# Hybrid SSD and GLA trunk, block 0: the third and the fourth GLA gate are projected in two steps instead of one

## The chip, the cores and the metric

The kernel runs on one core of a Trainium2 chip. The metric is the device time of one execution in microseconds (us), lower is better. Engines are named as in the profile: PE is the matrix engine, PEld its weight loads, DVE the vector engine, ACT the scalar engine, POOL the GpSimd engine, SP the engine that issues most of the DMAs.

## The reference

The reference is one decoder layer over 16 learned meta tokens and 2048 real tokens, width 1024, in float32. Cut to what matters here:

```python
u = rmsnorm(hres, norm_w)
proj = jnp.einsum('bld,dn->bln', u, w_in)
z, xbc, dt_raw, q, k, v, g_gla, a_lr, merge_g = split_cols(proj, IN_WIDTHS)
# branch 1 (SSD): short causal convolution and silu of xbc, chunked scan of 16 heads in 4 groups,
#                 times silu(z), RMSNorm per group
# branch 2 (GLA): 4 heads of gated linear attention in chunks
gate_logit = jnp.einsum('blr,rk->blk', a_lr, gla_gate_w2) + gla_gate_b
log_a = (jax.nn.log_sigmoid(gate_logit.astype(jnp.float32)) / GLA_GATE_TEMP)
# inside gla_chunked: gc = cumsum of log_a within a chunk
merged = jnp.sum(gates * branch_proj, axis=2)
return hres + jnp.einsum('bld,de->ble', merged, w_out)
```

The change concerns `gate_logit`: a rank-16 product per GLA head, its log-sigmoid and the cumulative sum in chunks.

## The kernel before, in words

The 2048 tokens are worked in four blocks of 512; block 0 also carries the 16 meta tokens (`m0` = 16), so it is 528 wide and most of its products are cut into two segments of 264 columns. Every large product is three matmuls (L214, L215, L216 in `accum`), because each operand is held as a high and a low part. After the blocks come the merge gates, the branch products and the output product; the change does not touch those.

Inside a block the work is a chain of **pieces**, and a piece is one projection or a half of one. For block 0 the chain is: `proj_zm` (steps 0 and 1), the convolution tiles of group 0 (steps 2 to 5), the z columns of group 1 in two halves (6, 7), the four convolution tiles of group 1 (8 to 11), z of group 2 (12, 13), the convolution tiles of group 2 (14 to 17), and so on; below, z of group 2 is the third z group. After each piece, `step()` advances every running generator by one `yield`: `gates` from step 6 on, and an `ssd_scan` for each group from steps 6, 12, 18 and 24 on. `gates` comes ahead of the scans in that list. The GLA scans that read the gates' result begin at step 30.

The order of instructions on PE and on the SP queue is this program order (`manual_schedule`). The order on DVE, ACT and POOL is chosen by the scheduler of the Tile framework when the kernel is built, and is then fixed; every engine works its queue in order. `tc.issue_after(x)` ties instructions behind `x` on their engine.

The accumulators lie in eight banks, in three pools: `pj` with three, `pt` with three and `pc` with two. What the steps around the change use:

- `proj_conv` (L585): one convolution tile takes two `pj` banks, one per segment. ACT evicts each bank twice (L595 into `cin`, L596 into `acc`), DVE adds three taps (L600), ACT takes a tanh (L603), DVE multiplies (L604). The matmuls of one tile run through both banks in turn.
- `proj_z` (L577): two `pj` banks over two steps; ACT takes the tanh of a bank (L516), DVE multiplies (L517).
- `gates` (L468): per head and segment one matmul (L488) with 48 rows, into a `pj` bank for the first segment and a `pt` bank for the second, each evicted by DVE (L490) and by ACT (L491). After a pair of heads come Exp (L493) and Ln (L494) over both, and then for each head a subtraction (L498) and the scans (L500). In block 0 these last are put off to the end of the step and tied behind the newest convolution tap or decay product (`convd`).
- `ssd_scan` (L618): `before(c)` transposes chunk `c` into a `pt` bank (L664), DVE takes three products from it (L667 to L670), ACT builds the decay (L677, L679), DVE masks it (L680). `after(c)`, one step later, multiplies with it on PE (L689, then L690 and L692 in two `pc` banks), and DVE adds up (L695 to L702). Step 11 runs `before(3)` and `after(2)` of group 0, step 12 `after(3)`; step 13 begins group 1's scan (L632, L648, L664).

Before the change, `gates` runs heads 0 and 1 together in step 7, and heads 2 and 3 together in step 11.

Of the kernel before, what the change touches and what calls it, by code (L numbers as in the profile page):

```python
# [43 lines left out]
def trunk_kernel(ctx: ExitStack, tc: tile.TileContext, xm, xmt, w_feat, w_tok, w_v3, w_zm, w_br, w_o,  # L44
# [7 lines left out]
    def mk(pool, shape, dt, tag, **kw):  # L52
        cnt[0] += 1
        return pool.tile(shape, dt, tag=tag, name=f"{tag}_{cnt[0]}", **kw)
# [77 lines left out]
    def bank(pool, tag):  # L132
        return mk(pool, [P, 512], F32, tag)
# [334 lines left out]
    def gates(o):  # L468
        m0, tt, chunks, g_all = o.m0, o.tt, o.chunks, o.g_all
        ast = (mk(wk, [P, META + BLK], F32R, "act", bufs=NACT) if m0 else mk(wk, [P, BLK], F32R, "sq", bufs=NSQ))[:48, :tt]  # L470
        for a, n in ([(0, META), (m0, BLK)] if m0 else [(0, BLK)]):
            ps = bank(pt, "pt")
            for i, (ca, cn) in enumerate(chunks):
                if a <= ca < a + n:
                    nc.tensor.transpose(ps[:48, ca - a:ca - a + cn], o.alr[:cn, i], ident[:cn, :cn])
            nc.scalar.activation(ast[:, a:a + n], ps[:48, :n], AF.Copy)
            nc.vector.tensor_tensor(ast[:32, a:a + n], ps[:32, :n], ast[:32, a:a + n].bitcast(F32),
                                    op=ALU.subtract)
            nc.scalar.activation(ast[:16, a:a + n], ps[:16, :n], AF.Copy)
        yield  # L480
        for h2 in range(0, GH, 2):
            gmt = mk(wk, [P, 2, META + BLK], F32, "tok4", bufs=NT4)
            for h in (h2, h2 + 1):
                gm = gmt[:, h % 2, :tt]
                gb = gate_b[:, h:h + 1]
                for i, (a, n) in enumerate(o.segs_all):
                    ps = bank(*((pj, "pj") if m0 and i == 0 else (pt, "pt")))
                    nc.tensor.matmul(ps[:, :n], w2[:, h * P:(h + 1) * P], ast[:, a:a + n],  # L488
                                     start=True, stop=True)
                    nc.vector.tensor_scalar(gm[:, a:a + n], ps[:, :n], gb, 0.0, op0=ALU.add, op1=ALU.min)  # L490
                    evicted[:] = [nc.scalar.activation(g_all[:, h, a:a + n], ps[:, :n], AF.Abs, bias=gb)]  # L491
            ga = g_all[:, h2:h2 + 2, :tt]
            nc.scalar.activation(ga, ga, AF.Exp, scale=-1.0)  # L493
            nc.scalar.activation(ga, ga, AF.Ln, bias=1.0)  # L494
            yield
            for h in (h2, h2 + 1):
                def sums(h=h):
                    nc.vector.tensor_tensor(gmt[:, h % 2, :tt], gmt[:, h % 2, :tt], g_all[:, h, :tt], op=ALU.subtract)  # L498
                    for a, n in chunks:
                        nc.vector.tensor_tensor_scan(g_all[:, h, a:a + n], ones[:, :n], gmt[:, h % 2, a:a + n], 0.0,  # L500
                                                     op0=ALU.mult, op1=ALU.add)

                if m0:
                    put_off.append(sums)
                else:
                    sums()
                yield
            if m0 and not h2:
                yield
# [494 lines left out]
    def enter(pieces, o):  # L1004
        b = o.b
        total = 6 * (SG + GH) + (b == nblk - 1)
        for n in range(total + 1):
            i, r = divmod(n, 6)
            if r == 0:
                if i == 1 and b == 0:  # L1010
                    begin(gates(o))
                if 0 < i <= SG:
                    begin(ssd_scan(o, i - 1))
                elif i > SG and not (b == nblk - 1 and i - SG > LATE_G):
                    begin(gla_scan(o, i - SG - 1))
                if (b, i) in beside:
                    begin(beside_unit(beside[b, i]))
            if b and n == 7:
                begin(gates(o))
            if n == 6 * SG + (3 if b else 0):  # L1020
                begin(fetch_u(b + 1) if b + 1 < nblk else first_b())
            if n < total:
                yield next(pieces)
        assert next(pieces, pieces) is pieces
# [502 lines left out]
```

## Time and profile before

| | |
|---|---|
| median of 3 runs | 2242.24 us (2240.61 to 2245.01) |
| the profiled execution | 2246.45 us, of which the span of the trace is 2244.7 us |
| PE busy | 2211.9 us, 99% of the span |
| DVE, ACT, POOL busy | 70%, 53%, 31% |
| mean granted clock of PE | 0.997 |
| DVE in block 0, from 90 to 110 us | 19.99 of 20 us |

PE's share is near the whole span, so what matters is where PE stands idle or runs slowly, and who makes it wait. In rows of the timeline the columns are start (us), duration (us), engine, line, operation, tiles written and read, and shapes; the brackets hold the idle time of the engine before the instruction and what ended it.

### The profile page before, as it was taken

The numbers are of one execution on the slowest core, as the hardware profiler recorded it, in microseconds if no ns is written. First come the engines' busy times: TensorE is split into PE (matmuls) and PEld (weight loads), VectorE is DVE, ScalarE is ACT, GpSimd is POOL, SyncE is SP. The second block draws the span as 40 slices with busy tenths as digits, with TensorE's granted clock in tenths as the row PEclk, the third lists the DMA queues.
The fourth block names the chain that finished last, engine by engine and source line by source line (L and its number), as shares of the span: only waits on it lengthen the run. The fifth ranks groups of instructions, "written<-read, shape, count | busy, mean of one in ns | idle before, by whom it ended". The sixth has DMA issues, their size and how long they took to land.

```text
span 2244.7 us, 34971 instructions
## 1 busy us (share of the span) xinstructions
PE 2211.9 (99%) x11789; PEld 1896.8 (85%) x11789; DVE 1577.0 (70%) x2935; ACT 1187.0 (53%) x2767; POOL 693.9 (31%) x689
## 2 busy tenths in 40 slices
PE   7999999999999999999999999999999999999998
PEld 7999999888888888888988888878888888888887
DVE  5775676677557676567677666674679945789866
ACT  5666655575445456544465544454644545454544
POOL 5444433223212122221212100066233374324341
PEclk9999999999999999999999999999999999999999
DMA  9767875767777667778667664376768866787753
GB/s 313 247 222 234 273 259 202 237 209 240 240 244 260 212 213 237 241 245 272 207 212 233 213 211 160 127 250 198 241 227 289 303 221 217 237 282 245 261 177 121
DMA packets 313699, 517.95 MB, mean 231 GB/s; under 512 B 28080, under 2 KB 162480, under 8 KB 313520
## 3 DMA queue, kind: packets, MB, share of 16 engines
q1 hardware_dynamic: 247008, 419.89, 57.8%
q10 hardware_dynamic: 65872, 93.74, 11.5%
q8 instruction: 92, 1.51, 0.3%
q0 software_dynamic: 640, 2.10, 0.2%
q14 instruction: 87, 0.71, 0.1%
HBM read 368.42 MB, written 147.19 MB: 230 GB/s over the span
## 4 chain that ended last, share of the span: by engine, by line
PE 89%; DVE 4%; DMA 3%; ACT 2%; issue 1%; POOL 1%; SPq 0%; POOLq 0%; ACTq 0%; DVEq 0%
PE pj L214 20%; PE pj L216 20%; PE pj L215 19%; PE pt L215 4%; PE pt L214 4%; PE pt L216 4%; PE pc L689 2%; PE pc L214 2%; PE pc L216 2%; PE pc L215 2%; PE pc L850 2%; PE pc L690 1%; DMA acc<-in_xmt 1%; PE pc L692 1%; PE pc L958 1%
## 5 line engine op out<-in xcount | busy, mean ns | idle before, releaser
L214 PE MATMUL pj<-ue,whl 128*128 128x264 f32 (+1 forms) x672 | 235.3, 350 | 1.9 <-ACT acc L596 1.2
L216 PE MATMUL pj<-ue,whl 128*128 128x264 f32 (+1 forms) x672 | 229.7, 342 | 0.0
L215 PE MATMUL pj<-ue,whl 128*128 128x264 f32 (+1 forms) x672 | 228.8, 340 | 0.0
L214 PE MATMUL pj<-uo,whl 128*128 128x512 f32 x512 | 205.7, 402 | 0.0
L216 PE MATMUL pj<-uo,whl 128*128 128x512 f32 x512 | 200.1, 391 | 0.0
L215 PE MATMUL pj<-uo,whl 128*128 128x512 f32 x512 | 199.5, 390 | 0.0
L214 PE MATMUL pj<-b,a 128*128 128x512 f32 (+1 forms) x484 | 188.9, 391 | 0.7 <-DVE io L1252 0.5
L216 PE MATMUL pj<-b,a 128*128 128x512 f32 (+1 forms) x484 | 188.9, 390 | 0.3 <-DVE a L1134 0.3
L215 PE MATMUL pj<-b,a 128*128 128x512 f32 (+1 forms) x484 | 187.6, 388 | 0.0
L600 DVE SCALAR_TENSOR_TENSOR acc<-cin,hcw,acc 128x512 f32<-128x512 f32 (+1 forms) x192 | 156.7, 816 | 39.7 <-ACT acc L596 38.6
L83 POOL TENSOR_TENSOR wr<-wr 128x256 f32<-128x256 f32 x80 | 66.0, 826 | 371.8 <-DMA wr<-y 158.1
L1124 POOL TENSOR_TENSOR as<-ar,ar 128x512 f32<-128x512 f32 x40 | 62.9, 1572 | 374.7 <-DMA ar<-in_w_br 179.9
L1134 DVE TENSOR_TENSOR a<-ar,a 128x512 fp32r<-128x512 f32 x160 | 130.8, 824 | 65.0 <-ACT a L1133 63.5
L1109 DVE TENSOR_TENSOR b<-br,b 128x512 fp32r<-128x512 f32 x140 | 128.9, 943 | 18.1 <-ACT b L1108 17.8
L214 PEld LDWEIGHTS pj<-ue,whl 128*128 128x128 f32 x672 | 126.2, 188 | 17.7 <-ACT acc L596 1.7
L216 PEld LDWEIGHTS pj<-ue,whl 128*128 128x128 f32 x672 | 126.4, 188 | 14.9
L215 PEld LDWEIGHTS pj<-ue,whl 128*128 128x128 f32 x672 | 126.4, 188 | 14.7
L177 POOL TENSOR_TENSOR whl<-wr,whl 128x512 fp32r<-128x512 f32 (+1 forms) x76 | 96.9, 1282 | 126.2 <-ACT whl L175 94.4
L1168 ACT ACTIVATE sn<-pj 128x512 f32<-128x512 f32 x118 | 70.0, 593 | 123.8 <-PE pj L216 70.8
L1134 DVE TENSOR_TENSOR a<-as,a 128x512 fp32r<-128x512 f32 x120 | 101.6, 848 | 45.2 <-ACT a L1133 42.5
L1133 ACT ACTIVATE a<-ar 128x512 fp32r<-128x512 f32 x160 | 99.0, 624 | 64.7 <-PE pt L216 30.2
L215 PE MATMUL pt<-b,a 128*128 128x512 f32 x320 | 125.6, 392 | 3.9 <-DVE b L1109 3.9
(329 smaller groups left out, 6467.6 us busy)
## 6 DMA issues: line engine op xcount, KB each, us to landing
whl<-k_s SPq DMA_DIRECT2D x96, 512.0 KB, 3.7
whl<-k_g SPq DMA_DIRECT2D x96, 512.0 KB, 4.3
whl<-k_v SPq DMA_DIRECT2D x36, 512.0 KB, 4.0
wr<-in_w_feat SPq DMA_DIRECT2D x64, 256.0 KB, 4.5
k_s<-whl SPq DMA_DIRECT2D x32, 512.0 KB, 3.9
cb<-cumd SPq DMA_DIRECT2D x64, 256.0 KB, 5.1
y<-gg ACTq DMA_DIRECT2D x64, 256.0 KB, 4.2
k_g<-whl SPq DMA_DIRECT2D x32, 512.0 KB, 4.0
```

The source lines that it names most:

```text
L83: nc.gpsimd.tensor_tensor(o, x, y, op=ALU.subtract)
L177: nc.gpsimd.tensor_tensor(hl[:, 1], raw, hl[:, 0].bitcast(F32), op=ALU.subtract)
L214: nc.tensor.matmul(ps, sh, mh, start=first, stop=False, **kw)
L215: nc.tensor.matmul(ps, sh, ml, start=False, stop=False, **kw)
L216: nc.tensor.matmul(ps, sl, mh, start=False, stop=last, **kw)
L600: convd[:] = [nc.vector.scalar_tensor_tensor(acc, cin[:, k:k + tt], hcw[:, ti, k:k + 1], acc, op0=ALU.mult, op1=ALU.add)]
L689: nc.tensor.matmul(py[:, h * 64:(h + 1) * 64], dm[:, h], xdt[:, h], start=True, stop=True)
L1109: nc.vector.tensor_tensor(t[:, 1], raw, t[:, 0].bitcast(F32), op=ALU.subtract)
L1124: nc.gpsimd.tensor_tensor(s1, a21, a22, op=ALU.add)
L1133: nc.scalar.activation(t[:, 0], src, AF.Copy)
L1134: latest[:] = [nc.vector.tensor_tensor(t[:, 1], src, t[:, 0].bitcast(F32), op=ALU.subtract)]
L1168: nc.scalar.activation(sn, self.ps[n, "a"], AF.Copy)
```

## The change

One `yield` is added in `gates`, which is reached in block 0 alone, between head 2 and head 3. Head 2 stays in step 11; head 3's matmuls and evictions, and the Exp and Ln over the pair, go to step 12; the put-off sums of heads 2 and 3 go from steps 12 and 13 to steps 13 and 14. No instruction is added or taken away.

```diff
                     nc.vector.tensor_scalar(gm[:, a:a + n], ps[:, :n], gb, 0.0, op0=ALU.add, op1=ALU.min)
                     evicted[:] = [nc.scalar.activation(g_all[:, h, a:a + n], ps[:, :n], AF.Abs, bias=gb)]
+                if m0 and h == 2:
+                    yield
             ga = g_all[:, h2:h2 + 2, :tt]
             nc.scalar.activation(ga, ga, AF.Exp, scale=-1.0)
             nc.scalar.activation(ga, ga, AF.Ln, bias=1.0)
```

## The prediction

> **What bounds the kernel now.** I read three views in this order: the matrix engine's (PE's) waits over the whole span, PE's timeline around the only long one in the first block, and the busy time and granted clock in the stretches of 3.41 us in which the clock changed. First the waits, longest in total on top: who waited and for whom, us in total, times, longest.
>
> ```profile
> core 0 of [0], span 2244.7 us
> engine line waited for: us in total, times, longest us
> PE pt L324 <- DMA cst<-in_cf: 10.1, 1, 10.1
> PE pt L215 <- DVE b L1109: 3.9, 3, 1.7
> PE pj L488 <- ACT acc L596: 3.1, 1, 3.1
> ```
>
> Behind the start-up load of 10.1 us PE hardly waits at all, so PE's own queue sets the end, and a microsecond that PE loses in block 0 is lost at the end. The third row is the one that the change touches. L488 is the gate matmul of `gates`, and it waits once in the kernel, for the eviction L596 of a convolution. PE's timeline (start, duration, line, tile, in brackets the idle time before it) shows which matmul, and what it costs behind it:
>
> ```profile
> 107.58 0.58 PE L488 MATMUL pj<-act,w 48*128 48x264 f32 x1 [3.15 <-ACT acc L596]
> ...
> 108.32 0.90 PE L664 MATMUL pt<-cst,act 128*128 128x128 f32 x3
> 109.01 1.80 PE L689 MATMUL pc<-c,sq 128*128 128x64 f32 x8
> ...
> 112.07 0.78 PE L214 MATMUL pj<-whl,ue 128*128 128x256 f32 x1
> ```
>
> This is step 11 (fourth convolution tile of group 1), then step 12 (first half of the third z group). In step 11 head 2's two matmuls run at once, in the third `pj` bank. Head 3's first matmul needs the first bank of the convolution tile that PE has only just finished, and stands from 104.43 to 107.58. Why that bank is late, on the scalar engine (ACT):
>
> ```profile
> 105.54 0.64 ACT L603 ACTIVATE act<-acc 128x528 f32<-128x528 f32 x1 [2.17 <-DVE acc L600]
> ...
> 106.97 0.56 ACT L596 ACTIVATE acc<-pj,hcb,hcw 128x264 f32<-128x264 f32 x1
> ...
> 107.69 0.58 ACT L596 ACTIVATE acc<-pj,hcb,hcw 128x264 f32<-128x264 f32 x1
> ```
>
> ACT works in order and was held by the tanh L603 of the tile before, which waited 2.17 us for the vector engine (DVE). Only then came the eviction of the first bank (ends 107.53) and of the second (ends 108.27). Now the clock (stretch, its length, busy time and count of PE, PEld, DVE, ACT, POOL, granted PE clock, DMA share, GB/s):
>
> ```profile
> 103.15:106.56 3.41, 1.29 (x10) 0.93 (x8) 3.41 (x8) 1.24 (x4) 0.00 (x0) 1.00 0.63 206
> 106.56:109.98 3.42, 2.40 (x11) 2.17 (x11) 3.41 (x7) 3.42 (x10) 2.83 (x3) 0.50 0.07 24
> 109.98:113.39 3.41, 3.41 (x13) 3.05 (x14) 3.24 (x8) 3.41 (x10) 1.26 (x2) 0.50 0.97 318
> ```
>
> The stall costs twice. After a stretch in which PE worked 1.29 of 3.41 us, the clock is 0.50 until 113.39. From 107.58 to 113.39 PE works 5.81 us at half speed, so about 2.9 us more are lost. The price of this place today is 3.15 + 2.9 = 6.05 us. Note also that DVE is busy for the whole of the first two stretches: behind PE's stall stands a full DVE.
>
> **The change, part by part.** The added `yield` leaves head 2 in step 11. Head 3's two matmuls, its two DVE evictions L490, its two ACT evictions L491, and the pair's Exp and Ln go to step 12, behind the first half of the third z group; the two sums go one step later too. `gates` issues no DMA, so no queue of SP or POOL is passed. Nothing is added or removed, only the order.
>
> *Step 11.* At 104.43 PE goes on to the three transposes L664; their `pt` bank was last used two transposes earlier. At half clock L664 to L689 took 109.01 - 108.32 = 0.69, so 0.35 at full clock: L689 could start at 104.78. It needs the decay tile that DVE finishes in L680:
>
> ```profile
> 105.76 0.68 DVE L680 TENSOR_TENSOR sq<-sq,sq 128x512 f32<-128x512 f32 x1
> ...
> 108.20 0.49 DVE L490 TENSOR_SCALAR tok<-pj,pv 128x264 f32<-128x264 f32 x1
> 108.61 0.48 DVE L490 TENSOR_SCALAR tok<-pt,pv 128x264 f32<-128x264 f32 x1
> 109.02 1.74 DVE L600 SCALAR_TENSOR_TENSOR acc<-cin,hcw,acc 128x528 f32<-128x528 f32 x1
> ...
> 115.20 0.68 DVE L680 TENSOR_TENSOR sq<-sq,sq 128x512 f32<-128x512 f32 x1
> ```
>
> The first L680 ends at 106.44 and stands in DVE's queue ahead of all that moves. So the wait of 3.15 us is not removed, it shrinks to 106.44 - 104.78 = 1.66 us at the next instruction group. Does an idle time of 1.66 us still cost the clock? The nearest rows are two later waits of 1.7 us (the L1109 row above), each in a stretch of its own:
>
> ```profile
> 1478.70:1482.10 3.40, 1.68 (x7) 1.05 (x6) 3.40 (x3) 2.44 (x5) 3.40 (x3) 1.00 0.59 196
> 1482.10:1485.50 3.40, 1.69 (x8) 1.35 (x8) 3.40 (x5) 0.00 (x0) 1.20 (x1) 1.00 0.31 85
> ```
>
> PE was busy for half of each, and the clock stayed at 1.00. I take it that the clock stays: 3.15 + 2.9 becomes 1.66. At full clock, the state product from L689 to the next projection and a half of z take, from the next step:
>
> ```profile
> 118.56 1.00 PE L689 MATMUL pc<-c,sq 128*128 128x64 f32 x8
> ...
> 120.12 0.47 PE L214 MATMUL pj<-whl,ue 128*128 128x256 f32 x1
> ...
> 126.00 0.49 PE L632 MATMUL pt<-cst,act 128*16 128x128 f32 x3
> ...
> 127.46 0.37 PE L214 MATMUL pj<-ue,whl 128*128 128x264 f32 x1
> ```
>
> 1.56 us and 5.88 us. So step 12 starts at 106.44 + 1.56 = 108.00 instead of 112.07, with its first bank evicted (107.53), and its first half of z ends at 113.88.
>
> *Step 12.* Head 3's pair took 108.32 - 107.58 = 0.74 at half clock, 0.37 at full, in the bank that head 2 left long before: 114.25. Then L689 of the last chunk, which stood at 118.56. PE would be 4.3 us early, but it needs the second L680 (115.20, end 115.88), and DVE has been full all the way. What moves that one forward: the two L490 of head 3 (0.82 us from 108.20 to 109.02) leave their place, but L600 cannot start before the second convolution eviction at 108.27, so 0.7 us are won; I allow another 0.15 for a small POOL wait on that path, which PE's earlier finish removes. L680 then ends at about 115.0. If the queue keeps head 3's L490 ahead of it, it ends at 115.88 as now; if its own inputs let it move further up, PE's 114.25 counts. Gain at this point: 2.7, 3.55 or 4.3 us. I take 3.6, because the rows tie L680 to DVE's queue and not to PE; the idle time left here is 0.7 us, less than the harmless 1.7.
>
> *Step 13 and 14.* The second half of z follows 1.56 us later and ends 5.88 us after that, at about 122.4. The convolution of group 2 begins 127.46 - 126.00 = 1.46 us behind it. Its banks are now both of z's, where before one was head 3's: with three banks taken in turn, removing head 3 from its place shifts z from banks 1 and 2 to 0 and 1, and the convolution again starts at 0. So its second bank has to be free a few tenths after 123.9. What stands in the way there:
>
> ```profile
> 126.19 0.60 ACT L516 ACTIVATE tok<-pj 128x512 f32<-128x512 f32 x1
> 126.86 0.67 DVE L517 SCALAR_TENSOR_TENSOR tok<-tok,pj 128x512 f32<-128x512 f32 x1
> ```
>
> Today the last bank of z is free at 127.53, 0.07 us after the convolution begins, and the convolution touches its second bank only after three matmuls. The cover is thin but there; I cost it at nothing, up to 0.5 us if the queues keep this order. The scans, 3.2 us of DVE each pair member, leave DVE's full stretch for one where it has idle time; their readers come in step 30. Gain 3.6 us, bounds of the working 2.0 to 4.3.
>
> The profiled execution took 2246.45 us (span 2244.7); the sum gives 2242.85 for it. The runs' median is 2242.24, 4.2 us lower, so I carry the difference over: 2238.6 us.
>
> **A rule weighed.** The Trainium skill (TensorE: Matmul & The Clock Gate, section "Part 1: The HAM clock gate") says that the clock falls to half after at least one whole idle window of about 3.4 us, and that the window runs freely and does not start with the kernel. Here it fell after a window in which PE was busy for 38%, so the trace does not bear out the first half; by it the stall would cost 3.15 us alone and the gain would be 0.85. The second half cannot be seen in one trace.
>
> **The rivals.**
> *No half clock in the timed runs.* If the stretches of 3.41 us fall so that the stall of 3.15 us is cut into two parts of less than 1.7 each, the clock stays. Then before reaches L689 of the last chunk at 107.58 + 0.37 + 0.35 + 1.56 + 5.88 = 115.74, held to 115.9 by L680, against 115.0 after: gain 0.9, 2241.3 us. Against it: only a small part of the positions does that, and this trace has the drop.
> *More than the forecast.* If L680's place moves up with PE, or the clock's low stretch lies wholly behind the stall in the usual run (6.83 us at half speed cost 3.4 and not 2.9), the gain goes to 4.3 + 0.5 = 4.8, and to the whole 6.05 if neither new wait comes: 2236.2 to 2237.4.
> *Slower: z's second bank.* The scalar engine's order is free, and head 3's Exp and Ln now come due between z's two tanhs:
>
> ```profile
> L494 ACT ACT_TABLE_LOAD  x8: 1283/1283/1283, 78.8 to 1193.5; - x8
> L494 ACT ACTIVATE g_all<-g_all x8: 1062/1062/1087, 80.1 to 1194.8; 128x1024 f32<-128x1024 f32 x6, 128x1056 f32<-128x1056 f32 x2
> ```
>
> Exp, table load, Ln and the load back are 1.06 + 1.28 + 1.06 + 1.28 = 4.7 us. Put behind the first tanh (PE is through with that bank at 119.5), they let the second start at 125.0 and free the bank at 126.3; PE wants it at about 124.3. Idle 2.0 us, more than the harmless 1.7, so 2.9 us at half clock may follow: 4.9 lost against 3.6 won, 2243.5 us. With a pair's scans of 3.2 us ahead of L517 too, 5.2 us are idle, 8.1 lost: 2246.7. It decides from a free second bank later than about 125. Against it: ACT had idle time before both tanhs, and the scans are tied behind a later L680.
> *The edit does nothing* is excluded: PE's order is the program's.
>
> **How the numbers follow.** Forecast 0.54, more 0.18, no half clock 0.10, slower 0.18. A measurement of this kernel tells about 0.2% (4.5 us) from no change; the line lies at 2237.76. The forecast's 3.6 is under it, but the low clock's position (up to 0.5 more) and the 4.3 bound reach it, and the rest of the schedule is planned anew around it; I put 0.22 of its 0.54 beyond the line. With "more" that is 0.40 faster. Of the slower case I put 0.15 beyond the line. The rest, 0.32 + 0.10 + 0.03 = 0.45, is the same. The range runs from the far end of "more", with 1 us for the spread of the runs, to the near end of the slower case: 2235.2 to 2243.5; outside lie most of the slower case and a little below.
>
> **What would show it.** Right: no wait of L488 for L596 any more; a wait of about 1.7 us of L689 for L680 in step 11 and one under 1 us in step 12; no stretch at 0.50 near 107; step 12 starting about 4 us earlier and the convolution of group 2 about 3.6. Wrong: a wait of L214 in the first matmuls of the group 2 convolution for L516 or L517, a clock of 0.50 there, or a second L680 that still ends at 115.9.

## The result and the profile after

| | before | after |
|---|---|---|
| median | 2242.07 us of 22 runs (2240.21 to 2245.01) | 2239.38 us of 22 runs (2236.72 to 2241.49) |
| profiled execution | 2246.45 us, span 2244.7 | 2241.24 us, span 2239.5 |
| PE idle at the place of the change | 3.15 us | 1.56 us |
| head 2's first gate matmul to the first projection of group 2 | 23.53 us | 19.65 us |

The ratio of after to before is 0.9986, 95% interval [0.998, 0.9992]: a gain of about 3.1 us (1.8 to 4.5). It is clear of zero, and under the 0.2% that the prediction called a measurable difference. One run of before, taken beside three of the later kernels, was in a slow state (5084.73 us) and is left out of their ratios. Two added lines push every later line number up by two: L596 of before is L598 of after, L689 is L691, L680 is L682, L516 and L517 are L518 and L519.

The distance in the last row of the table is used in all that follows. It begins with the last pair of matmuls ahead of the change (head 2's first L488: 103.93 before, 102.78 after) and ends where step 14 begins (127.46 and 122.43). So it leaves out the start of the kernel, which differs by 1.15 us between these two executions, and also a wait inside step 14.

PE's waits after, longest in total on top (who waited for whom, us in total, times, longest):

```profile
PE pt L324 <- DMA cst<-in_cf: 10.0, 1, 10.0
PE pt L215 <- DVE b L1111: 3.1, 2, 1.7
PE pc L214 <- DVE c L948: 2.6, 4, 0.8
PE pc L691 <- DVE sq L682: 1.6, 1, 1.6
```

No gate matmul waits for a convolution's eviction any more. In its place stands one wait of 1.6 us of the state product L691 for the decay tile L682. PE's timeline after:

```profile
102.78 0.39 PE L488 MATMUL pj<-act,w 48*128 48x264 f32 x1
103.01 0.28 PE L488 MATMUL pt<-act,w 48*128 48x264 f32 x1
103.22 0.55 PE L666 MATMUL pt<-cst,act 128*128 128x128 f32 x3
105.32 1.10 PE L691 MATMUL pc<-c,sq 128*128 128x64 f32 x8 [1.56 <-DVE sq L682]
...
107.00 0.47 PE L214 MATMUL pj<-whl,ue 128*128 128x256 f32 x1
...
112.97 0.39 PE L488 MATMUL pj<-act,w 48*128 48x264 f32 x1
113.19 0.28 PE L488 MATMUL pt<-act,w 48*128 48x264 f32 x1
113.40 1.10 PE L691 MATMUL pc<-c,sq 128*128 128x64 f32 x8
```

Head 3's pair now runs at 112.97 behind the first half of z, and neither it nor the L691 behind it waits. The two L682 of DVE, and what stands between them:

```profile
104.59 0.68 DVE L682 TENSOR_TENSOR sq<-sq,sq 128x512 f32<-128x512 f32 x1
...
106.95 0.41 DVE L669 TENSOR_TENSOR c<-pt,tkd 128x256 f32<-128x256 f32 x1
107.28 0.41 DVE L671 TENSOR_TENSOR c<-pt,wde 128x256 f32<-128x256 f32 x1
107.61 0.41 DVE L672 TENSOR_TENSOR tok<-pt,pv 128x256 f32<-128x256 f32 x1
107.94 1.66 DVE L602 SCALAR_TENSOR_TENSOR acc<-cin,hcw,acc 128x528 f32<-128x528 f32 x1
...
112.25 0.68 DVE L682 TENSOR_TENSOR sq<-sq,sq 128x512 f32<-128x512 f32 x1
112.85 0.41 DVE L704 TENSOR_TENSOR tok<-c,tok 128x256 f32<-128x256 f32 x1
```

The first ends at 105.27, and 0.05 us later L691 starts: that wait belongs to DVE's queue. Behind the gate's two L490 stand now the three products from the last chunk's transposes, ahead of the tap L602, where before the tap came first; and L704, which as L702 of before stood ahead of the second decay tile, stands behind it. Now the clock, in the stretches of 3.41 us in which the wait lies (columns as in the prediction). The clock does not change here, so the stretches are counted back, in steps of 3.413 us, from its fall at 2234.61, behind the last matmul:

```profile
101.28:104.69 3.41, 2.49 (x18) 1.97 (x17) 3.41 (x9) 1.12 (x3) 0.00 (x0) 1.00 0.83 270
104.69:108.10 3.41, 2.78 (x20) 2.68 (x21) 3.41 (x9) 3.41 (x10) 2.13 (x3) 1.00 0.00 0
```

The boundary at 104.69 cuts the idle time in two, PE worked 73% of the first stretch and 81% of the second, and the clock stayed at 1.00. In this execution, then, the place got 3.88 us shorter: 1.59 us less idle time, and 2.3 us for the most part from the half clock that is gone.

### The profile page after: what moved, and what is told of

Same layout as the page of the kernel before. It is cut to its first block, busy times and chain, and to the rows that moved or that the text cites. A ratio compares the mean times of both kernels' runs of the same rounds, so it can differ in the third digit from the quotient of the medians.

```text
span 2239.5 us, 34970 instructions
## 1 busy us (share of the span) xinstructions
PE 2209.3 (99%) x11789; PEld 1894.2 (85%) x11789; DVE 1577.6 (70%) x2935; ACT 1187.4 (53%) x2767; POOL 694.8 (31%) x689
## 4 chain that ended last, share of the span: by engine, by line
PE 86%; DMA 6%; DVE 4%; ACT 2%; issue 1%; SPq 1%; POOL 0%; POOLq 0%; ACTq 0%; DVEq 0%
PE pj L214 19%; PE pj L216 19%; PE pj L215 19%; PE pt L215 4%; PE pt L214 4%; PE pt L216 4%; PE pc L691 2%; PE pc L214 2%; PE pc L216 2%; PE pc L215 2%; PE pc L852 2%; DMA acc<-in_xmt 2%; PE pc L692 1%; DMA br<-gate_t 1%; PE pc L694 1%; PE pc L960 1%
## 5 line engine op out<-in xcount | busy, mean ns | idle before, releaser
L602 DVE SCALAR_TENSOR_TENSOR acc<-cin,hcw,acc 128x512 f32<-128x512 f32 (+1 forms) x192 | 158.3, 824 | 39.6 <-ACT acc L598 38.3
L1136 DVE TENSOR_TENSOR a<-as,a 128x512 fp32r<-128x512 f32 x120 | 107.1, 894 | 46.3 <-ACT a L1135 43.3
L1111 DVE TENSOR_TENSOR b<-br,b 128x512 fp32r<-128x512 f32 x140 | 123.6, 906 | 19.8 <-ACT b L1110 19.0
```

The costliest lines, as they stand in the source:

```text
L602: convd[:] = [nc.vector.scalar_tensor_tensor(acc, cin[:, k:k + tt], hcw[:, ti, k:k + 1], acc, op0=ALU.mult, op1=ALU.add)]
L1111: nc.vector.tensor_tensor(t[:, 1], raw, t[:, 0].bitcast(F32), op=ALU.subtract)
L1136: latest[:] = [nc.vector.tensor_tensor(t[:, 1], src, t[:, 0].bitcast(F32), op=ALU.subtract)]
```

## The experiments

Theory: the gain comes from the place of head 3's matmuls in PE's queue; they no longer wait for a bank, and the clock is spared. Rivals: it comes from the relief of DVE and ACT in the full stretch; or the half clock is without weight in the usual run.

### Only the later work of ACT and DVE is moved

```diff
+            if m0 and h2:
+                yield
             ga = g_all[:, h2:h2 + 2, :tt]
```

> The kernel before, with only the Exp, the Ln and the two put-off sums of heads 2 and 3 one step later; all four gate matmuls stay together in step 11. Theory (the gain comes from the matmul's place on PE): the wait of 3.1 us of the gate matmul for the convolution's eviction and the half clock stay, distance 23.5, time as before within 0.5 us. Rival (the gain comes from taking ACT and DVE work out of the full stretch): the distance falls by 1 us or more, the time by as much.

The ratio to before is 1.0000 [0.9992, 1.0009], and PE's wait stands as it was:

```profile
PE pj L488 <- ACT acc L598: 3.1, 1, 3.1
```

Moving Exp, Ln and the sums alone brings nothing that can be measured. The distance was 22.45 us and not 23.53, with the same idle time: here the clock was at 0.50 for one stretch of 3.41 us, and in the profile of before for two. Half of 3.41 is 1.7 us; 1.08 was seen, and why it is less was not traced.

### Only PE's order is moved

Head 3 resumes at the end of step 11, behind the state product (the last two lines stand in `step()`, behind the loop over the generators); all else stays in its step.

```diff
+                if m0 and h == 2:
+                    again.append(1)
+                    yield
...
+        while again:
+            next(again.pop())
```

> Head 3's two matmuls are issued behind the state product of step 11 and not in step 12; Exp, Ln and sums stay in the steps of before. Theory: head 3 finds its bank free at once, only the wait of about 1.6 us for the decay tile is left, the clock stays at 1.00, distance 19.6 to 20.5 (the second decay tile may come up to 0.9 us later, since head 3's evictions are back in DVE's full stretch). Time 2 to 3 us under before, as the change. Rival (the sums' later step and the evictions' later place matter): distance 22 or more.

The ratio is 0.9993 [0.9985, 1.0002], the median 1.4 us under before. The wait of the gate matmul is gone and a wait of 1.56 us for the decay tile is what is left, as expected. But the distance was 22.69 us, for a reason that I had not expected: the clock fell.

```profile
102.93:106.34 3.41, 1.85 (x14) 1.48 (x15) 3.41 (x9) 1.97 (x6) 0.63 (x1) 1.00 0.49 171
106.34:109.75 3.41, 3.41 (x11) 2.35 (x11) 3.41 (x7) 3.41 (x12) 3.14 (x4) 0.50 0.35 118
```

Here the idle time lay wholly inside one stretch. PE worked 54% of it, more than in the two later stretches at 49% that the prediction had leaned on, and the next two stretches ran at half clock. Without those 6.83 us at half speed the distance would be about 22.69 - 3.4 = 19.3, so the order on PE alone gives the gain of idle time. The fall is not an accident of this one execution: over the 11 timed runs the mean granted clock is 0.9980, near that of before (0.9978) and under that of the changed kernel (0.9988). So with head 3's pair in step 11 the half clock is hardly spared, and this kernel does not show whether its place behind dense matmuls, in step 12, is what spares it.

### The changed kernel once more

> The changed kernel once more, beside the other two: wait of 1.56 us again, at the same place, 2.5 to 3.5 us under before. Theory (the stretches of 3.41 us run freely): the wait lies elsewhere in its stretch, and if it lies wholly inside one the clock may be 0.50 behind it, with a distance of 21 to 22.7 instead of 19.65. Rival: the clock is 1.00 here in every execution, since 1.6 us are too short for it.

The same program, the same wait (1.57 us), and a distance of 21.28 us instead of 19.65:

```profile
106.22 1.35 PE L691 MATMUL pc<-c,sq 128*128 128x64 f32 x8 [1.57 <-DVE sq L682]
...
108.83 0.78 PE L214 MATMUL pj<-whl,ue 128*128 128x256 f32 x1
```

```profile
103.52:106.93 3.41, 1.84 (x13) 1.32 (x12) 3.41 (x8) 1.67 (x5) 0.33 (x1) 1.00 0.58 197
106.93:110.34 3.41, 3.41 (x14) 3.05 (x14) 3.41 (x7) 3.41 (x11) 3.14 (x4) 0.50 0.26 88
```

So one and the same program pays for the clock here in one execution and not in the other. What differs is where the stretch begins: at 104.69 it cut the wait in two, here the wait lies wholly between 103.52 and 106.93. One stretch at half clock cost 1.63 us, which is half of 3.41 but for the last tenth. The ratio to before was 0.9991 [0.9981, 1.0], in the interval of the first measurement. Over the timed runs the mean granted clocks tell how often it happens: 0.9978 in 33 runs of before, 0.9988 in the first 22 runs of the changed kernel, 0.9985 in these 11. Weighted, that is 0.0009 of 2240 us, some 2 us of PE's time; against the runs of before that were taken beside these 11 (0.9979) it is some 1.2 us. So 1 to 2 of the 3.1 us gained are the clock's, by a rough split: the clocks are recorded to three places, and every trace here also ends with 2 to 5 us at 0.50 behind the last matmul, which cost PE nothing and are in each mean. Kernels below whose profile has no other fall have a mean of 0.9991. The Trainium skill (TensorE: Matmul & The Clock Gate, section "Part 1: The HAM clock gate") has the window run freely and not start with the kernel; these two traces agree, with 19.65 and 21.28 us for one program.

A second thing is seen by matching these two executions instruction by instruction. The first was 2.5 us ahead from step 14 on, and 1.6 us behind at the end: it lost 4.1 us at a few later places, the largest lasting shifts at 1046 to 1056 (1.35 us), at 1440 to 1485 (1.15) and near 703 (1.06). The same program moves by more than the whole gain. So single times say little here, and I read each experiment by its distance and by its interval.

### Useless matmuls in the wait

If the clock is the larger part, work that does nothing should help. First, in the kernel before, head 2's second matmul 25 times into its own bank:

```diff
-                    nc.tensor.matmul(ps[:, :n], w2[:, h * P:(h + 1) * P], ast[:, a:a + n],
-                                     start=True, stop=True)
+                    for _ in range(25 if m0 and h == 2 and i else 1):
+                        nc.tensor.matmul(ps[:, :n], w2[:, h * P:(h + 1) * P], ast[:, a:a + n],
+                                         start=True, stop=True)
```

> The kernel before, with head 2's second matmul of step 11 issued 25 times into its own bank (the same values): about 24 x 0.12 = 2.9 us of useless work on PE inside the wait of 3.15 us. Distance from head 2's first gate matmul to the first projection of group 2: 23.5 us before, 19.65 us after the change. Theory (the wait costs twice, once as idle time and once as half clock): the clock stays at 1.00, the distance falls by about 2.7 us to 20.8, the time by about 2.7 us, although work was added. Rival (the half clock costs nothing that the full DVE queue would not take anyway): the distance stays at 23.5 and the time is that of before.

Slower: 1.0013 [1.0004, 1.0022], distance 23.83. PE was busy for the whole stretch, and the clock fell all the same:

```profile
103.00:106.42 3.42, 3.42 (x28) 3.31 (x26) 3.42 (x8) 1.72 (x5) 0.39 (x1) 1.00 0.37 130
106.42:109.83 3.41, 3.40 (x16) 2.86 (x15) 2.87 (x4) 1.90 (x5) 3.10 (x3) 0.50 0.28 93
```

These matmuls have 48 of 128 rows. So the same with matmuls on all 128 rows, into the bank that head 3's second segment overwrites:

```diff
+                spare = bank(pt, "pt") if m0 and h == 3 else None
+                if spare is not None:
+                    for _ in range(24):
+                        nc.tensor.matmul(spare[:, :264], o.u[0][:, 0, :P], o.u[0][:, 0, :264], start=True, stop=True)
```

> The kernel before, with 24 useless matmuls on all 128 rows between head 2 and head 3 of step 11, into the bank that head 3's second segment overwrites (24 x 0.12 = 2.9 us inside the wait of 3.15 us). The filler on 48 rows kept PE busy for the whole of a stretch and the clock fell all the same. Theory (the clock follows how much of the array works, and the half clock is a part of the price): it stays at 1.00 near 107 us, the distance from head 2's first gate matmul to group 2's first projection falls from 23.5 to about 20.8, and the time by 1.5 to 2.5 us (the half clock costs the timed runs 2.2 us more before than after the change, by their mean clocks). Rival (the half clock costs nothing that DVE's full queue would not take anyway): distance over 22.5, time as before.

```profile
101.78:105.19 3.41, 3.41 (x27) 3.13 (x26) 3.41 (x8) 0.91 (x3) 0.00 (x0) 1.00 0.90 291
105.19:108.61 3.42, 3.36 (x28) 3.00 (x26) 3.31 (x7) 3.42 (x10) 2.19 (x2) 1.00 0.09 32
```

The clock held at this place, and the mean clock of the timed runs rose to 0.9989. Yet the time did not fall: 1.0011 [1.0002, 1.002], and the distance was 24.2 us. Step 12 started after 6.05 us instead of 8.14, but then the scheduler had put all three taps ahead of head 3's evictions on DVE, the second decay tile was begun 1.6 us later behind head 2's first matmul than before (12.89 and 11.27 us), and the product stood waiting for it:

```profile
117.11 1.10 PE L693 MATMUL pc<-c,sq 128*128 128x64 f32 x8 [1.54 <-DVE sq L684]
```

Behind that wait the clock fell after all, at 118.84. The 2.1 us were given back, and more, to a wait that the new order on DVE made. The rival has the distance (over 22.5) but not the reason: PE came to this product 12.10 us behind head 2's first matmul (117.11 - 1.54 - 103.47), and in the order of before the tile was done at 11.95, so in that order it would not have waited. A filler that makes the scheduler plan anew is not a clean test of what the half clock costs. Last, 12 such matmuls inside the wait that the change leaves:

```diff
             py = bank(pc, "pc")
+            if m0 and not g and c == 2:
+                for _ in range(12):
+                    nc.tensor.matmul(py[:, :264], o.u[0][:, 0, :P], o.u[0][:, 0, :264], start=True, stop=True)
```

> The changed kernel, with 12 useless matmuls on 128 rows (1.4 us) ahead of the state product of chunk 2, inside the wait of 1.56 us that the change leaves, into a bank that the product overwrites. Theory (the wait of 1.56 us still drops the clock in some runs, by where the stretches of 3.41 us fall, as in the profile with head 3 behind the state product): mean clock up, distance 19.6 to 19.9, time 0.5 to 1.5 us under the changed kernel. Rival (the changed kernel does not lose clock here): the time is that of the changed kernel.

The mean clock rose from 0.9988 to 0.9991 and the distance was 19.64, both as expected; the time was not under the changed kernel's (0.9993 [0.9984, 1.0002], the changed kernel 0.9986). In its profile group 2's first projection waited 1.1 us for L519, z's product, at its second bank. Whether the filler is worth anything stays open.

### The state product one step later

```diff
+            if m0 and not g and c == NCH - 1:
+                yield
             if m0 and c > 1:
                 square(c - 2)
             after(c - 1)
```

> The changed kernel, with the state product of chunk 2 of group 0's scan one more step later (behind the first half of z instead of ahead of it), so that the decay tile has 6 us more. Theory (what is left of the stall is the wait of 1.56 us for the decay tile): that wait goes, distance 19.65 - 1.56 = 18.1, time 1.5 us under the changed kernel. Rival (DVE is full, the wait comes again one step later): distance 19.6, time as the changed kernel.

A miss, and neither theory's: 0.9997 [0.9989, 1.0006], distance 22.79. With the state product out of the way, z follows head 2 at once and wants the convolution's first bank itself:

```profile
106.51 0.39 PE L214 MATMUL pj<-whl,ue 128*128 128x256 f32 x1 [2.66 <-ACT acc L598]
```

A stretch at half clock follows (0.50 from 107.50 to 110.92). In each order of PE's queue that was run (before, the change, head 3 behind the state product, and this one) the next instruction that needs something from DVE or ACT waits for their late stretch; the order chooses which instruction does.

### Taking load from DVE instead

Head 1's sums (a subtraction and five scans) are held in a list, and put off in step 12 and not in step 9. In the first two of these kernels the sums read the second pair's buffer, so head 1's decay is computed from other data; the instructions are the same. The cut shows the changed kernel; in the kernel before the list is emptied where head 2's sums are put off, in step 12 too.

```diff
                 if m0 and h == 2:
                     yield
+                    put_off.append(held_sums.pop())
...
-                if m0:
+                if m0 and h == 1:
+                    held_sums.append(sums)
+                elif m0:
                     put_off.append(sums)
```

> The kernel before, with the sums of head 1 (a subtraction and five scans, 3.2 us of DVE) put off from step 9 to step 12; PE's order is that of before. Theory (the bank is late because DVE is full in steps 8 to 11): the wait of 3.15 us falls under 0.5 us, no half clock, distance 17.5 to 19, time 4 to 6 us under before. Rival (the bank is late by ACT's order and not by DVE's load): a wait of 2 us or more stays, and the time is within 1 us of before.

> The changed kernel with the same putting off of head 1's sums. Theory: the wait of 1.56 us for the decay tile goes too, distance about 18, time 1.5 to 2.5 us under the changed kernel, and equal to the kernel before with head 1's sums put off within 1 us. Rival (the scans then delay the next tile and a wait comes back in steps 12 to 14): time as the changed kernel.

The kernel before with this edit: 0.9981 [0.9972, 0.999], distance 17.98, no wait of the gate matmul. The changed kernel with it: 0.9973 [0.9963, 0.9983], distance 17.82, no wait over 0.4 us in steps 11 to 14, the lowest median of all (2236.99, of 9 runs). Then with head 1's own buffer:

```diff
-                def sums(h=h):
+                def sums(h=h, gmt=gmt):
```

> The kernel before, with head 1's sums put off from step 9 to step 12, now on head 1's own buffer (in the run before they read the second pair's buffer, so that head 1's decay came from other data; the work was the same). PE's order is that of before. Theory (DVE's load makes the bank late): no wait of the gate matmul over 0.5 us, no half clock near 107, distance 17.5 to 18.5, time 3 to 5 us under before. Rival (on its own buffer the subtraction waits for data that were late before too): a wait of 1.5 us or more stays in step 11.

> The changed kernel with the same putting off, on head 1's own buffer. Theory: no wait over 0.4 us in steps 11 to 14, distance 17.8 to 18.2, time 2 to 3 us under the changed kernel, so 5 to 6 us under before. Rival (the sums, one place earlier in DVE's queue than in the run before, delay head 3's eviction or z's product): a wait of 0.5 to 1.5 us at the first matmul of group 2, time 1 us under the changed kernel.

The kernel before, so edited: 0.9986 [0.9977, 0.9995], distance 17.98. All four gate matmuls stand together in step 11 as before, and the eviction comes right behind the tile, without the delay of 3 us:

```profile
103.20 0.39 ACT L597 ACTIVATE cin<-pj 128x264 f32<-128x264 f32 x1 [0.55 <-PE pj L216]
103.49 0.56 ACT L598 ACTIVATE acc<-pj,hcb,hcw 128x264 f32<-128x264 f32 x1
```

So the late bank is DVE's doing: take head 1's sums from steps 9 to 11 (in the trace of before 3.6 us of DVE, from 95.58 on), and the change isn't needed. It is as good as the change, not better, though its distance is 1.7 us shorter; 0.81 us go to a wait of group 2's first projection for z's product, inside step 14, and the rest is less than the runs can tell. The changed kernel with the relief, 0.9991 [0.9983, 1.0], has that wait larger:

```profile
120.77 0.37 PE L214 MATMUL pj<-ue,whl 128*128 128x264 f32 x1
...
123.31 0.54 PE L214 MATMUL pj<-ue,whl 128*128 128x264 f32 x1 [1.92 <-DVE tok L522]
```

and a stretch at 0.50 behind it. This is the mechanism of the prediction's slower rival. On ACT:

```profile
117.15 1.07 ACT L496 ACTIVATE g_all<-g_all 128x1056 f32<-128x1056 f32 x1
118.25 1.28 ACT L497 ACT_TABLE_LOAD   x1
119.54 1.08 ACT L497 ACTIVATE g_all<-g_all 128x1056 f32<-128x1056 f32 x1
120.64 1.28 ACT L521 ACT_TABLE_LOAD   x1
121.94 0.60 ACT L521 ACTIVATE tok<-pj 128x512 f32<-128x512 f32 x1
```

Exp, table load, Ln and the load back stand ahead of both tanhs of z. So they do in the changed kernel, where Exp starts at 115.54, 12.76 us behind head 2's first matmul, and nobody waits. Here it starts 14.20 us behind it (117.15 - 102.95), because head 3's evictions were queued behind the scans of head 1. In the kernel with the foreign buffer the scans came behind those evictions, Exp started after 10.48 us, and the wait was not there.

### Exp and Ln behind z's tanhs

```diff
+            if m0 and h2:
+                yield
+            with behind() if m0 and h2 else nullcontext():
                 nc.scalar.activation(ga, ga, AF.Exp, scale=-1.0)
                 nc.scalar.activation(ga, ga, AF.Ln, bias=1.0)
```

(on the kernel just told of)

> The changed kernel with head 1's sums put off to step 12, and with the Exp and Ln of heads 2 and 3 tied behind the second tanh of z's third group (step 13), the sums behind them one step later. Theory: in the run before, Exp, Ln and their two table loads (4.7 us) stood ahead of z's tanhs on ACT and made group 2's first projection wait 1.92 us and lose a stretch of clock; behind the tanhs they delay nobody. No wait over 0.4 us in steps 11 to 14, no half clock there, distance 17.8, time 2 to 3 us under the changed kernel, 5 to 6 us under before. Rival (they then hold up the decay of group 1's scan on ACT, whose exponential needs the table back): a wait of 1 us or more in steps 14 or 15, and the time of the changed kernel.

Steps 11 to 13 went as the theory has it: no wait, distance 17.83. The rival was right about what follows. The table loads now hold up the decay and the scaling of the scan on ACT, and PE stops in step 14:

```profile
130.03 0.33 PE L745 MATMUL pt<-cst,tok 128*128 128x128 f32 x1 [1.94 <-ACT tok L738]
```

with a stretch at half clock behind it, though PE worked 70% of the stretch ahead of the fall:

```profile
129.22:132.64 3.42, 2.39 (x11) 1.33 (x11) 0.56 (x1) 3.42 (x10) 1.46 (x2) 1.00 0.32 127
132.64:136.05 3.41, 3.41 (x16) 3.41 (x17) 3.32 (x4) 1.68 (x4) 1.60 (x1) 0.50 0.85 289
```

The ratio to before is 0.9998 [0.9989, 1.0007]. Of the 5.7 us by which the distance is shorter than before, 3.6 are given back there (1.94 idle, 1.7 of clock); where the rest went is not traced. A version that keeps head 1's scans behind head 3's evictions on its own buffer would be the next to try; it was not run. None of the kernels on each head's own buffer was faster than the change.

## Why the prediction was right, and where it was not

- **The price of the place** was 3.15 us idle and, by the two distances, 2.3 us at half clock, where 2.9 were worked out; what is left of the idle time was forecast as 1.66 and measured as 1.56. The wait was not removed; it moved to L689, as worked out.
- **Step 12** starts 4.21 us behind head 2's first matmul where it was 8.14: 3.93 us earlier, forecast 4.07.
- **The second decay tile** was forecast to end 0.9 us earlier, and to leave PE 0.7 us of waiting. It came 1.8 us earlier (112.93 - 102.78 = 10.15 behind head 2's first matmul, before 115.88 - 103.93 = 11.95), and PE did not wait. The term that was mis-sized is the order on DVE, which I kept as it was: the forecast has 0.7 us for head 3's two L490 and 0.15 for POOL. Beyond that, the product L704 went behind the decay tile (as L702 it held it for 0.34 us, from 114.86 to 115.20), and some 0.35 us of small gaps between DVE's instructions on that path went too. The three products that now fill the place ahead of the tap, which waits for ACT, save only about 0.1. At this point PE gained 4.01 us (14.63 us from head 2's first matmul to the last chunk's state product before, 10.62 after): its own pace, nearer to the far bound (4.3) than to the value taken (3.6). Over the whole distance it is 3.88. The rows of before, which now stand the other way round:

```profile
114.86 0.43 DVE L702 TENSOR_TENSOR tok<-c,tok 128x256 f32<-128x256 f32 x1
115.20 0.68 DVE L680 TENSOR_TENSOR sq<-sq,sq 128x512 f32<-128x512 f32 x1
```

- **Z's second bank** did not hold PE up: group 2's projection began at 122.43 without a wait. But the banks were misread. The prediction has both banks of that tile as z's, the second free only after z's second product. In the changed kernel with the relief the tile's first matmuls start at 120.77, ahead of both tanhs of z (121.94 and 122.95), so its first bank is not one of z's; the fourth matmul, the first into the second bank, waits for z's first product alone. By that product the cover was 3.25 us before (free at 124.66, wanted at 127.91) and 1.24 us in the changed kernel:

```profile
120.96 0.69 DVE L519 SCALAR_TENSOR_TENSOR tok<-tok,pj 128x512 f32<-128x512 f32 x1 [3.34 <-ACT tok L518]
...
122.89 0.28 PE L214 MATMUL pj<-ue,whl 128*128 128x264 f32 x1
```

- **"I take it that the clock stays"** is the step that failed. It was right in the profiled execution, by the position of the stretch, and wrong in the second one and with PE's order alone. The nearest rows that I chose, two waits of 1.7 us at 49% busy, were near in idle time and not in kind: there PE worked with matmuls of 128 rows by 512 columns, here with gates on 48 rows, transposes and products of 64 columns. A price that hangs on the position should have been a mean over positions, on both sides: before was priced with 2.9 us and paid 2.3 in its trace, after was priced with 0 and pays 0 in one execution and 1.6 in the next. Both errors make the forecast gain too large; by the mean clocks the clock's part is 1 to 2 us and not 2.9. That the time came out, 2239.38 for 2238.6, is in part luck: the value taken for the second decay tile was 0.4 us too small, which works the other way, and the interval of the gain (1.8 to 4.5 us) does not tell 3.6 from 3.1.
- **The rivals.** The timed runs of before do not lack the half clock: their mean clock is 0.9978, where kernels without a fall in block 0 have 0.9991. The order that the slower rival feared came true and more, for Exp, Ln and the two table loads stand ahead of both tanhs of z (115.54 to 120.31); its wait did not, since the bank that counts had 1.24 us of cover. Four of the other kernels have a wait at that place: 1.92 us in the changed kernel with the relief, 1.11 with the filler in the changed kernel, and 0.85 and 0.81 in the two kernels of before with the relief.

## What to carry to other kernels

When an engine waits for a bank, ask what keeps the one who frees it: here DVE was full (19.99 of 20 us from 90 to 110), and each of four orders of PE's queue met that stretch with a wait (of L488, twice of the state product for its decay tile, and of z's first matmul). Moving the instruction is worth the difference between its wait and the next one, which can be read from the row that ends last. And a stall of about half a stretch (1.56 of 3.41 us) has to be priced by its chance of lowering the clock, since the same idle time cost 0 in one execution and 1.6 us in the next.

## What the runs showed of the hardware

The granted clock does not follow the share of time in which PE is busy. It fell behind a stretch that was filled with matmuls on 48 rows (3.42 of 3.42 us busy), behind stretches that were busy for 54% with gates, transposes and products of 64 columns, behind one that was busy for 70%, with eight transposes and two products behind a wait (Exp and Ln behind z's tanhs), and held through stretches of matmuls of 128 rows by 512 columns that were busy for 49%. With the filler on all 128 rows it held. Every fall in block 0 lasted one or two stretches of 3.41 us (3.413 and 6.827), and the same program had one in one execution and none in the other. That the clock weighs how much of the array works is argued from these cases; no run measured it by itself. The Trainium skill (TensorE: Matmul & The Clock Gate, section "Part 1: The HAM clock gate") ties the fall to a whole idle window of about 3.4 us, which none of these falls had.
